# First norm of a macaron block: sums of squares by ScalarE over turned tokens, root on four numbers per token, spread by one product

## The chip, the core and the metric

One core of a Trainium2 chip runs the whole program; the other seven are idle. The metric is the device time of one execution in microseconds (us). The core's engines work through their own lists of instructions in order and meet at semaphores: PE (TensorE) multiplies matrices into PSUM, DVE (VectorE) and ACT (ScalarE) do the elementwise work, POOL (GpSimd) a little of it, and SP (SyncE) issues the DMA transfers.

## What is computed

One layer on 1,024 tokens of width 1,024, in float32: a half-step feed-forward block, a mixing part (short convolution and differential attention), a second half-step feed-forward block, and a last norm. The change touches the first lines only:

```python
def rms_norm(x, g):
    xf = x.astype(jnp.float32)
    y = xf * lax.rsqrt(jnp.mean(xf * xf, axis=-1, keepdims=True) + NORM_EPS)
    return (y * g.astype(jnp.float32)).astype(x.dtype)

def swiglu(x, w_gate, w_up, w_down):
    return (jax.nn.silu(x @ w_gate) * (x @ w_up)) @ w_down

h = h + 0.5 * swiglu(rms_norm(h, norm_ffn1[l]), ffn1_gate[l], ffn1_up[l], ffn1_down[l])
```

x is (1, 1024, 1024), the gate and up weights are (1024, 2816), the down weight (2816, 1024).

## The kernel before

The features lie on the partitions and the tokens along the free axis. The 1,024 tokens are two halves `t` of 512 and the 1,024 features two halves `o` of four blocks of 128, so the input is four tiles `h[o][t]` of 128 x 4 x 512. A product in float32 is made of three quick ones: each operand is split into a rounded part `hi` (an ACT copy) and the rest `lo` (a DVE subtraction), and hi x hi, hi x lo and lo x hi are summed in PSUM. A group is twelve such products of 128 x 128 by 128 x 512 (four blocks of features, three products each).

The width 2,816 of the feed-forward is worked in eleven steps `j` of 256 columns, gate and up together. Step 0 is written out by hand in `Start`, and its order on PE, DVE, ACT and POOL is the order of the code. It starts before the norm is known: `operand` multiplies x by the gain alone (ACT gives `hi`, DVE `lo`), `weights` splits a block of weights, `mm` adds one group of products, and only `ev` multiplies a finished sum in PSUM by the norm's factor `r[t]` of each token. There are sixteen groups, for gate and up (`x`), two column halves (`o`), two token halves (`t`) and two feature halves (`kk`). `squares` and `norm` make `r[t]`: ACT squares the eight 128 x 512 pieces of a token half, DVE adds them up (`add_square`), PE multiplies the sum with a matrix of ones, which adds over the partitions and gives every partition the result, and `rstd` takes the reciprocal root (one ACT operation, then three DVE operations of 128 x 512). `apply` (line 651) multiplies x by gain and `r[t]`: four DVE operations for each of the four tiles. These normed tiles are what all later steps multiply.

From step 1 on `pair_jobs` makes seven products in place of eight out of sums of quarters (a Strassen-like scheme): for each of gate and up the products come in the order `ORDER = (2, 1, 7, 6, 4, 5, 3)`, and each of them needs a block `B(i)`, a sum of normed tiles split into `hi` and `lo`. Products 1, 6, 5 and 3 are added one after the other onto one PSUM bank, 7 onto a second and 2 and 4 onto a third and back; after each of them the bank's value is taken out before the next product is added onto it:

```python
if (o, t) not in C:
    C[o, t] = self.C()
    nc.scalar.copy(C[o, t], ps)
else:
    nc.vector.tensor_tensor(C[o, t], C[o, t], ps, ALU.add)
```

The copy is line 308 (ACT), the addition line 310 (DVE). So product 6 can't begin until the addition of product 1 has read the bank, and that addition adds onto what the copy of product 2 took out. Outside the hand-written stretch the scheduler of the compiler sets the order of each engine's list. PSUM tiles are named `sc` (two tiles of two banks), `at` (two of one bank), `ps` and `ot` (one each); in SBUF, `Q` are the large tiles, `A` and `F` split weights, and `C` pieces of 128 x 512.

Of the kernel before, what the change touches and what calls it, by code (L numbers as in the profile page):

```python
# [25 lines left out]
EPS = 1e-6  # L26
# [34 lines left out]
class Operands:  # L61


    def __init__(self, k):
        self.k = k
        self.made = {}
        self.left = {}
# [62 lines left out]
class Stream(Operands):  # L130
# [29 lines left out]
class K:  # L160
# [293 lines left out]
    def setup(self):  # L454
        nc = self.nc
        self.cst = self.t("cst", [P, C_N])
        nc.sync.dma_start(self.cst, self.io["consts"])
        self.ones = self.t("ones", [P, P])
        nc.vector.memset(self.ones, 1.0)
        self.eps = self.t("eps", [P, 1])  # L460
        nc.vector.memset(self.eps, EPS)
        self.ng = self.t("ng", [P, 32])
        nc.vector.tensor_scalar(self.ng, self.cst[:, 0:32], -1.0, None, ALU.mult)

    def ffn_loads(self, wg, wu):
        return [self.load_raw(wg[0]), self.load_raw(wu[0])]
# [126 lines left out]
class Start:  # L593


    def __init__(self, k, x, wg, wu, gd):
        nc = k.nc
        self.k, self.gd = k, gd
        self.h = [[None, None], [None, None]]
        raws = [k.t("Q", [P, 2, 8, P]) for _ in range(2)]  # L600
        self.st, self.r, self.s, self.A, self.acc, self.G = {}, {}, {}, {}, {}, {}
        self.B = Blocks(k, 4)
        self.B.q = self.h
        dma = nc.sync.dma_start
        for kk in range(2):
            q = slice(4 * kk, 4 * kk + 4)
            h = self.h[kk][0] = k.t("Q", [P, 4, TH])
            dma(h[:, 0:2], x[kk][0][:, 0:2])
            dma(raws[0][:, 0, q], wg[:, 0, q])
            dma(h[:, 2:4], x[kk][0][:, 2:4])  # L610
            dma(raws[0][:, 1, q], wg[:, 1, q])
            for o in range(2):
                dma(raws[1][:, o, q], wu[:, o, q])
            self.s[kk, 0] = k.t("Q", [P, 4, TH], F32R), k.t("Q", [P, 4, TH], F32R)
        for kk in range(2):
            self.h[kk][1] = k.t("Q", [P, 4, TH])
            dma(self.h[kk][1], x[kk][1])
            self.s[kk, 1] = k.t("Q", [P, 4, TH], F32R), k.t("Q", [P, 4, TH], F32R)
        self.raws = raws
# [12 lines left out]
            nc.scalar.activation(hi[:, j], src, AF.Copy, scale=self.gain(o, j))  # L632
            nc.vector.scalar_tensor_tensor(lo[:, j], src, self.gain(o, j), hi[:, j].bitcast(F32), ALU.mult, ALU.subtract)

    def squares(self, o, t):
        k, nc = self.k, self.k.nc
        for j in range(4):
            sq = k.C()
            nc.scalar.activation(sq, self.h[o][t][:, j], AF.Square)
            k.add_square(self.st, t, sq)  # L640

    def norm(self, t):
        k, nc = self.k, self.k.nc
        ps = self.sc[1][:, :TH] if t == 0 else k.ps("at")
        nc.tensor.matmul(ps, k.ones, self.st[t][0], start=True, stop=True)
        self.r[t] = k.rstd(ps, D, TH)

    def apply(self, t, o):
        for j in range(4):
# [9 lines left out]
    def mm(self, x, o, t, kk):  # L659
        k = self.k  # L660
        if kk == 0:
            if t == 1 and x == 0:
                self.acc[x, o] = self.sc[1 - o][:, TH:]
            else:
                self.acc[x, o] = k.ps({(0, 1, 0): "ps", (0, 1, 1): "ot", (1, 1, 1): "ps"}.get((t, x, o), "at"))
        ps, a, (hi, lo) = self.acc[x, o], self.A[x, o, kk], self.s[kk, t]
        for q in range(4):
            for n, (y, z) in enumerate(((0, hi), (0, lo), (1, hi))):
                k.nc.tensor.matmul(ps, a[:, y, q], z[:, q], start=kk == q == n == 0, stop=kk == 1 and q == 3 and n == 2)

    def ev(self, x, o, t):
        k, nc = self.k, self.k.nc
        c = k.C()
        nc.vector.scalar_tensor_tensor(c, self.acc.pop((x, o)), -1.0, self.r[t], ALU.mult, ALU.mult)
        if x == 0:
            nc.scalar.activation(c, c, AF.Silu)
            self.G[o, t] = c
        else:
            g = self.G[o, t]
            k.tt(g, g, c, ALU.mult)  # L680
            k.finished(self.G, o, t, self.gd, 0)

    def run(self, load):
        k = self.k
        XO = [(0, 0), (0, 1), (1, 0), (1, 1)]
        B = self.B.get

        self.sc = [k.ps("sc"), k.ps("sc")]
        for _ in range(self.WARM):
            k.nc.tensor.matmul(self.sc[0][:, :P], k.ones, k.ones, start=True, stop=True)  # L690
        self.operand(0, 0, (0, 1))
        self.weights(0, 0, 0)
        self.operand(0, 0, (2, 3))
        self.mm(0, 0, 0, 0)
        for x, o in XO[1:]:
            self.weights(x, o, 0)
            self.mm(x, o, 0, 0)
        self.squares(0, 0)
        self.operand(1, 0, range(4))
        for o in range(2):  # L700
            self.weights(0, o, 1)
        self.mm(0, 0, 0, 1)
        self.squares(1, 0)
        for o in range(2):
            self.weights(1, o, 1)
        self.operand(0, 1, range(4))
        self.squares(0, 1)
        self.norm(0)
        self.mm(0, 1, 0, 1)
        self.operand(1, 1, range(4))  # L710
        self.squares(1, 1)
        raws = load()
        self.mm(1, 0, 0, 1)
        self.ev(0, 0, 0)
        self.ev(0, 1, 0)
        self.mm(1, 1, 0, 1)
        self.ev(1, 0, 0)
        self.ev(1, 1, 0)
        for x, o in XO[:2]:
            self.mm(x, o, 1, 0)  # L720
        self.apply(0, 0)
        self.norm(1)
        for x, o in XO[2:]:
            self.mm(x, o, 1, 0)
        B(1)
        self.apply(0, 1)
        self.mm(*XO[0], 1, 1)
        B(2)
        for x, o in XO[1:]:
            self.mm(x, o, 1, 1)  # L730
        self.apply(1, 1)
        for x, o in XO:
            self.ev(x, o, 1)
        self.apply(1, 0)
        self.B.plan(7)
        return raws

# [23 lines left out]
class Mixer:  # L761
# [10 lines left out]

    def constants(self):
        k, nc = self.k, self.k.nc
        self.ident = k.t("ident", [P, P])
        make_identity(nc, self.ident)

        mm = k.C()
        nc.gpsimd.memset(mm[:, 0:192], 0.0)
        nc.gpsimd.memset(mm[0:1, 0:64], 1.0)  # L780
        nc.gpsimd.memset(mm[0:1, 128:192], NEG_BIG)
        self.mask = k.t("msk", [P, 192], F32R)
        nc.vector.tensor_copy(self.mask, mm[:, 0:192])

        lam = k.C()
        lv = k.C()[:, 0:256]
        nc.sync.dma_start(lv, k.io["lambdas"])
        nc.vector.tensor_tensor(lam[:, 0:64], lv[:, 0:64], lv[:, 64:128], ALU.mult)
# [667 lines left out]
```

## Time and profile before

| | us |
|---|---|
| median of 3 runs (lowest, highest) | 2081.24 (2080.03, 2082.38) |
| the profiled execution, its own time | 2082.11 |
| its span from first to last instruction | 2080.3 |
| PE busy (share of the span) | 1981.0 (95%) |
| DVE busy | 1402.0 (67%) |
| ACT busy | 935.1 (45%) |

The times are of unprofiled executions, the rest is from one profiled execution; its own time is 1.8 us longer than its span. A busy share is a mean over the whole span and doesn't say what happens in the first 110 us, where the change lies. The granted clock of PE was 0.978 of 2.4 GHz on average.

### The profile page before, as it was taken

Reading aid. Unit: us, or ns where it says so; the run is one execution under the profiler, and the core shown is the slowest. Engines: PE = TensorE matmul, PEld = TensorE weight load, DVE = VectorE, ACT = ScalarE, POOL = GpSimd, SP = SyncE. Lnnn points to the kernel's source line nnn. Section 1 sums busy time; section 2 is a strip of 40 time slices with the busy share of each in tenths; the row PEclk is TensorE's granted clock in tenths of the full one; section 3 lists DMA queues with packets and bytes.
Section 4 is the critical chain, followed back from the end, with each engine's and each line's share of the span. In section 5 each row is a group of like instructions: output and inputs, shape, how many; then the busy total and the mean of one; then the engine's idle time right before and its main releaser. Section 6 shows DMA issues by size and latency. Waiting matters only on the chain.

```text
span 2080.3 us, 24145 instructions
## 1 busy us (share of the span) xinstructions
PE 1981.0 (95%) x8808; PEld 1624.7 (78%) x8808; DVE 1402.0 (67%) x2166; ACT 935.1 (45%) x1684; POOL 136.8 (7%) x123
## 2 busy tenths in 40 slices
PE   9799999999999999999799997999999999999997
PEld 8588888888877877777578775877788888888885
DVE  8965665676866856656376737798865665666874
ACT  7433333353464633233366656456433333353362
POOL 0000000000000000000244445000000000000000
PEclk9899999999999999999899998999999999999998
DMA  5223223264543423312333344423223223274441
GB/s 213 84 109 113 95 102 117 81 236 159 194 157 111 152 98 100 126 57 71 119 105 122 97 148 144 190 81 132 97 102 121 86 101 112 82 264 152 150 154 59
DMA packets 81208, 259.70 MB, mean 125 GB/s; under 512 B 10048, under 2 KB 16320, under 8 KB 63936
## 3 DMA queue, kind: packets, MB, share of 16 engines
q1 hardware_dynamic: 81088, 258.15, 34.8%
q8 instruction: 69, 1.13, 0.2%
q14 instruction: 51, 0.42, 0.1%
HBM read 183.14 MB, written 74.97 MB: 124 GB/s over the span
## 4 chain that ended last, share of the span: by engine, by line
PE 81%; DVE 10%; ACT 3%; issue 2%; POOL 1%; DMA 1%; SPq 0%; DVEq 0%; ACTq 0%; POOLq 0%
PE sc L267 37%; PE at L267 16%; PE ps L267 9%; PE ot L267 8%; DVE Q L243 3%; PE ps L1159 2%; DVE A L243 1%; DVE C L243 1%; DVE F L243 1%; PE ps L1221 1%; PE sc L955 1%; PE sc L339 1%; PE sc L338 1%; PE sc L337 1%; PE sc L1221 1%
## 5 line engine op out<-in xcount | busy, mean ns | idle before, releaser
L267 PE MATMUL sc<-Q,A 128*128 128x512 f32 x1968 | 473.5, 390 | 2.4 <-ACT C L308 2.4
L267 PEld LDWEIGHTS sc<-Q,A 128*128 128x128 f32 x1968 | 369.7, 188 | 81.3 <-ACT C L308 3.2
L267 PE MATMUL sc<-Q,F 128*128 128x512 f32 x1548 | 382.1, 396 | 29.5 <-ACT Q L248 11.4
L267 PEld LDWEIGHTS sc<-Q,F 128*128 128x128 f32 x1548 | 294.6, 191 | 96.9 <-ACT Q L248 12.9
L243 DVE TENSOR_TENSOR F<-Q,F 128x512 fp32r<-128x512 f32 (+1 forms) x307 | 211.8, 696 | 170.1 <-ACT F L248 169.7
L248 ACT CAST F<-Q 128x512 fp32r<-128x512 f32 (+1 forms) x315 | 190.0, 612 | 256.5 <-PE sc L267 88.1
L243 DVE TENSOR_TENSOR Q<-Q,Q 128x512 fp32r<-128x512 f32 (+4 forms) x334 | 278.7, 887 | 33.6 <-ACT Q L248 26.8
L248 ACT CAST A<-Q 128x512 fp32r<-128x512 f32 (+1 forms) x299 | 180.3, 611 | 268.0 <-PE sc L267 159.1
L243 DVE TENSOR_TENSOR A<-Q,A 128x512 fp32r<-128x512 f32 (+1 forms) x299 | 202.0, 678 | 130.2 <-ACT A L248 129.3
L267 PE MATMUL at<-Q,F 128*128 128x512 f32 x1128 | 279.4, 393 | 10.1 <-ACT C L308 9.2
L267 PEld LDWEIGHTS at<-Q,F 128*128 128x128 f32 x1128 | 213.0, 189 | 57.3 <-ACT C L308 10.9
L248 ACT CAST Q<-Q 128x512 fp32r<-128x512 f32 (+1 forms) x214 | 153.1, 759 | 87.0 <-DVE Q L243 31.1
L243 DVE TENSOR_TENSOR C<-C,C 128x512 f32<-128x512 f32 x236 | 161.5, 688 | 16.6 <-DMA C<-zd 5.0
L243 DVE TENSOR_TENSOR Q<-Q 128x512 f32<-128x512 f32 x216 | 148.3, 690 | 3.7
L267 PE MATMUL ps<-Q,A 128*128 128x512 f32 x498 | 124.2, 390 | 0.0
L308 ACT COPY C<-sc 128x512 f32<-128x512 f32 x88 | 51.4, 588 | 156.5 <-PE sc L267 155.4
L267 PE MATMUL ot<-Q,A 128*128 128x512 f32 x450 | 112.8, 392 | 0.9 <-DVE Q L398 0.9
L267 PEld LDWEIGHTS ps<-Q,A 128*128 128x128 f32 x498 | 93.6, 188 | 19.6 <-issue 0.3
L1159 PE MATMUL ps<-Q,F 128*128 128x512 f32 x384 | 105.9, 412 | 3.1 <-ACT C L1165 3.1
L267 PE MATMUL at<-Q,A 128*128 128x512 f32 x444 | 107.6, 389 | 0.8 <-DVE C L310 0.8
L310 DVE TENSOR_TENSOR C<-C,sc 128x512 f32<-128x512 f32 x81 | 55.6, 687 | 75.3 <-ACT C L308 35.1
L267 PEld LDWEIGHTS ot<-Q,A 128*128 128x128 f32 x450 | 85.3, 190 | 19.0 <-issue 1.3
(218 smaller groups left out, 2190.6 us busy)
## 6 DMA issues: line engine op xcount, KB each, us to landing
Q<-in_ffn_gate SPq DMA_DIRECT2D x21, 1024.0 KB, 5.8
Q<-in_ffn_up SPq DMA_DIRECT2D x21, 1024.0 KB, 4.8
Q<-in_w_in SPq DMA_DIRECT2D x20, 1024.0 KB, 5.4
g1d<-C SPq DMA_DIRECT2D x77, 256.0 KB, 2.0
g2d<-C SPq DMA_DIRECT2D x77, 256.0 KB, 2.0
Q<-in_ffn_down SPq DMA_DIRECT2D x16, 1024.0 KB, 6.5
Q<-g1d SPq DMA_DIRECT2D x14, 1024.0 KB, 6.3
Q<-g2d SPq DMA_DIRECT2D x14, 1024.0 KB, 5.8
```

The source lines that it names most:

```text
L243: e.tensor_tensor(out, a, b, op)
L248: self.nc.scalar.copy(hi, src)
L267: mm = lambda *x, **kw: self.nc.tensor.matmul(*x, skip_group_check=True, **kw)
L308: nc.scalar.copy(C[o, t], ps)
L310: nc.vector.tensor_tensor(C[o, t], C[o, t], ps, ALU.add)
L337: mm(ps, a[:, 0, q], hi[:, q], start=n == q == 0, stop=False)
L338: mm(ps, a[:, 0, q], lo[:, q], start=False, stop=False)
L339: mm(ps, a[:, 1, q], hi[:, q], start=False, stop=n == 1 and q == 3)
L955: nc.tensor.matmul(sc[:, a : a + w], qs[:, hl, s, qb * P : (qb + 1) * P], kst[:, s, a : a + w], start=hl == 0, stop=hl == 1 and a + w < n)
L1159: nc.tensor.matmul(ps, a[kk][:, x, q], y[:, q], start=c == 0, stop=c == 23)
L1221: nc.tensor.matmul(ps, a[:, x, kk], b[:, y, kk % 2], start=c == 0, stop=c == 11)
```

## The change

`squares` no longer squares the pieces as they lie. PE turns them first (a transpose of 128 x 128 by the unit matrix `ident`, which is now made at the start), so that 128 tokens lie on the partitions and their 1,024 features along the free axis of one `sc` tile; one ACT operation squares the 1,024 values of each token and sums them into one number. There are eight such steps, four blocks `b` of 128 tokens for each half `t`, with eight turns each. `root` takes the reciprocal root on 128 x 4 numbers (one ACT and four small DVE operations) and then ACT multiplies `ident` by the four columns (four operations of 128 x 128) into a tile `diag`. `norm` multiplies this tile with the matrix of ones, which gives all partitions the factor of each token, and ACT copies it out of PSUM. The order of `run` is another one: all eight groups of the first token half and all turns come before the first `ev`.

```diff
-    def squares(self, o, t):
-        for j in range(4):
-            sq = k.C()
-            nc.scalar.activation(sq, self.h[o][t][:, j], AF.Square)
-            k.add_square(self.st, t, sq)
+    def squares(self, t, b):
...
+        tp = k.ps("sc")
+        for o in range(2):
+            for j in range(4):
+                c = (4 * o + j) * P
+                nc.tensor.transpose(tp[:, c : c + P], self.h[o][t][:, j, b * P : (b + 1) * P], k.ident)
+        nc.scalar.activation(self.junk, tp, AF.Square, accum_out=self.w[t][:, 0, b : b + 1])
+
+    def root(self, t):
+        ss, y, v, a, r = (self.w[t][:, i] for i in range(5))
+        nc.scalar.activation(y, ss, AF.Abs_reciprocal_sqrt, bias=k.eps, scale=1.0 / D)
+        nc.vector.tensor_scalar(v, ss, 0.5 / D, 0.5 * EPS, ALU.mult, ALU.add)
+        nc.vector.tensor_tensor(a, y, y, ALU.mult)
+        nc.vector.tensor_tensor(v, a, v, ALU.mult)
+        nc.vector.scalar_tensor_tensor(r, v, -1.5, y, ALU.add, ALU.mult)
+        d = self.diag[t] = k.C()
+        for b in range(4):
+            nc.scalar.activation(d[:, b * P : (b + 1) * P], k.ident, AF.Copy, scale=r[:, b : b + 1])
 
     def norm(self, t):
         ps = self.sc[1][:, :TH] if t == 0 else k.ps("at")
-        nc.tensor.matmul(ps, k.ones, self.st[t][0], start=True, stop=True)
-        self.r[t] = k.rstd(ps, D, TH)
+        nc.tensor.matmul(ps, k.ones, self.diag[t], start=True, stop=True)
+        self.r[t] = k.C()
+        nc.scalar.copy(self.r[t], ps)
...
         self.mm(0, 0, 0, 1)
-        self.squares(1, 0)
+        self.squares(0, 0)
+        self.squares(0, 1)
         for o in range(2):
             self.weights(1, o, 1)
+        self.mm(0, 1, 0, 1)
+        self.squares(0, 2)
+        self.squares(0, 3)
         self.operand(0, 1, range(4))
-        self.squares(0, 1)
+        self.root(0)
+        self.mm(1, 0, 0, 1)
+        self.squares(1, 0)
+        self.squares(1, 1)
+        self.operand(1, 1, range(4))
+        self.mm(1, 1, 0, 1)
+        self.squares(1, 2)
+        self.squares(1, 3)
+        raws = load()
+        self.sc = [k.ps("sc"), k.ps("sc")]
         self.norm(0)
-        self.mm(0, 1, 0, 1)
-        self.operand(1, 1, range(4))
-        self.squares(1, 1)
-        raws = load()
-        self.mm(1, 0, 0, 1)
-        self.ev(0, 0, 0)
-        self.ev(0, 1, 0)
-        self.mm(1, 1, 0, 1)
-        self.ev(1, 0, 0)
-        self.ev(1, 1, 0)
+        self.root(1)
         for x, o in XO[:2]:
             self.mm(x, o, 1, 0)
+        for x, o in XO:
+            self.ev(x, o, 0)
+        for x, o in XO[:2]:
+            self.mm(x, o, 1, 1)
+        self.apply(0, 1)
+        B(2)
+        self.mm(*XO[2], 1, 0)
+        self.norm(1)
...
```

What this does to the lists of the engines is seen at three places. Names are tile kinds with running numbers, and the numbers differ between the two programs.

On PE before, the product with ones for the first token half (line 645) stands between the fifth and the sixth group of `Start`:

```order
L669 MATMUL at_22_156<-Q_12_114,F_33_236 128x512
L669 MATMUL at_22_156<-Q_11_113,F_33_236 128x512
L645 MATMUL sc_20_124<-C_29_217,ones_2_87 128x512
L669 MATMUL at_24_172<-Q_11_113,A_34_239 128x512
L669 MATMUL at_24_172<-Q_12_114,A_34_239 128x512
```

On PE now, the same product (line 668, on the tile `diag`) stands behind the eighth group (`ot`, line 693) and the last sixteen of the 64 turns (line 648):

```order
L693 MATMUL ot_28_208<-Q_13_119,A_36_272 128x512
L693 MATMUL ot_28_208<-Q_12_118,A_36_272 128x512
L648 MATMUL sc_43_378<-ident_5_93,Q_14_120 128x128 x4
L648 MATMUL sc_43_378<-ident_5_93,Q_17_124 128x128 x4
L648 MATMUL sc_44_388<-ident_5_93,Q_14_120 128x128 x4
L648 MATMUL sc_44_388<-ident_5_93,Q_17_124 128x128 x4
L668 MATMUL sc_48_403<-C_39_320,ones_2_87 128x512
L693 MATMUL sc_48_403<-Q_15_122,F_21_153 128x512
```

The product moved behind three more groups and all turns, and its PSUM tile `sc_48` lies where `sc_43` lay, so it waits for the square of that tile.

On DVE before, the end of the first half's norm (lines 437 to 439), the operand of the last tile (633), the last additions of squares (243 on `C`) and the first `ev` (674):

```order
L437 SCALAR_TENSOR_TENSOR C_46_293<-sc_20_124,C_45_292 128x512
L438 TENSOR_TENSOR C_46_293<-C_46_293,C_45_292 128x512
L439 SCALAR_TENSOR_TENSOR C_46_293<-C_46_293,C_45_292 128x512
L633 SCALAR_TENSOR_TENSOR Q_18_122<-Q_16_119,cst_1_85,Q_17_121 128x512 x4
L243 TENSOR_TENSOR C_41_280<-C_41_280,C_47_318 128x512
L243 TENSOR_TENSOR C_41_280<-C_41_280,C_48_321 128x512
L243 TENSOR_TENSOR C_41_280<-C_41_280,C_49_324 128x512
L243 TENSOR_TENSOR C_41_280<-C_41_280,C_50_327 128x512
L674 SCALAR_TENSOR_TENSOR C_53_346<-at_22_156,C_46_293 128x512
```

On DVE now, the same place, with the first `ev` in line 698:

```order
L635 SCALAR_TENSOR_TENSOR Q_19_127<-Q_17_124,cst_1_85,Q_18_126 128x512 x4
L656 TENSOR_SCALAR tn_40_337<-tn_40_337 128x4
L657 TENSOR_TENSOR tn_40_337<-tn_40_337 128x4
L658 TENSOR_TENSOR tn_40_337<-tn_40_337 128x4
L659 SCALAR_TENSOR_TENSOR tn_40_337<-tn_40_337 128x4
L698 SCALAR_TENSOR_TENSOR C_51_441<-at_22_160,C_49_405 128x512
```

The additions and the wide root are gone; the small root of the second token half (its inputs are the last squares) now stands ahead of the first `ev`.

On DVE before, the first two additions of line 310, those of product 1 in step 1, with `apply` of the last tile (line 651) ahead of them and the making of `B(7)` (243 on `Q`) behind:

```order
L243 TENSOR_TENSOR C_72_525<-C_54_349,C_71_524 128x512
L651 SCALAR_TENSOR_TENSOR Q_13_115<-Q_13_115,ng_4_91,C_59_403 128x512 x4
L310 TENSOR_TENSOR C_81_572<-C_81_572,sc_86_598 128x512
L310 TENSOR_TENSOR C_84_591<-C_84_591,ps_90_632 128x512
L243 TENSOR_TENSOR Q_13_115<-Q_16_119,Q_13_115 128x512 x4
```

On DVE now, the same two additions:

```order
L243 TENSOR_TENSOR C_68_583<-C_63_553,C_51_441 128x512
L243 TENSOR_TENSOR Q_103_818<-Q_8_102,Q_102_817 128x512 x3
L243 TENSOR_TENSOR Q_107_867<-Q_17_124,Q_106_866 128x512 x4
L243 TENSOR_TENSOR Q_103_818<-Q_8_102,Q_102_817 128x512
L243 TENSOR_TENSOR C_69_584<-C_52_444,C_68_583 128x512
L310 TENSOR_TENSOR C_78_627<-C_78_627,sc_83_653 128x512
```

They stand behind the making of all the blocks (`Q_103` and `Q_107` are the `lo` parts of `B(5)` and `B(3)`, the last two). Between the first `ev` and the first of these additions there were 62 DVE instructions, and now there are 96.

## Rows read from the trace of the kernel before

**Rows 1.** The page: the chain that ended last, shares of the span by engine.

```profile
PE 81%; DVE 10%; ACT 3%; issue 2%; POOL 1%; DMA 1%; SPq 0%; DVEq 0%; ACTq 0%; POOLq 0%
```

**Rows 2.** Busy us by engine (xinstructions) in stretches; PE's granted clock, DMA share, GB/s.

```profile
70.00:80.00 10.00, 1.22 (x2) 0.50 (x2) 9.97 (x17) 3.26 (x6) 0.00 (x0) 0.60 0.21 79
80.00:90.00 10.00, 9.53 (x31) 7.69 (x32) 10.00 (x18) 5.87 (x11) 0.00 (x0) 0.72 0.07 26
100.00:400.00 300.00, 300.00 (x1325) 248.51 (x1324) 188.02 (x290) 108.81 (x190) 0.00 (x0) 1.00 0.29 109
```

**Rows 3.** The chain that ended last, in order of time: start us, us, what.

```profile
7.71 0.65 DVE Q L633
...
79.80 0.63 ACT Q L248
```

**Rows 4.** Timeline of PE: start us, us, instruction, [idle before <- releaser].

```profile
20.33 2.88 PE L669 MATMUL at<-Q,F 128*128 128x512 f32 x12
...
26.64 2.88 PE L669 MATMUL ps<-Q,F 128*128 128x512 f32 x12
29.36 2.88 PE L669 MATMUL ot<-Q,A 128*128 128x512 f32 x12
...
77.45 0.79 PE L267 MATMUL sc<-Q,F 128*128 128x512 f32 x1 [9.39 <-ACT Q L248]
```

**Rows 5.** Timeline of DVE.

```profile
18.82 3.08 DVE L243 TENSOR_TENSOR C<-C,C 128x512 f32<-128x512 f32 x4
...
35.56 1.28 DVE L674 SCALAR_TENSOR_TENSOR C<-at,C 128x512 f32<-128x512 f32 x2
...
40.69 2.73 DVE L651 SCALAR_TENSOR_TENSOR Q<-Q,ng,C 128x512 f32<-128x512 f32 x4
...
43.34 0.69 DVE L437 SCALAR_TENSOR_TENSOR C<-at,C 128x512 f32<-128x512 f32 x1
...
74.87 0.68 DVE L310 TENSOR_TENSOR C<-C,sc 128x512 f32<-128x512 f32 x1
...
79.08 14.53 DVE L243 TENSOR_TENSOR Q<-Q,Q 128x512 f32<-128x512 f32 x24
```

**Rows 6.** Products of line 267, the first 180 of them: PE, PEld, clock, DMA.

```profile
54.70:112.30 57.60, 44.39 (x180) 35.41 (x180) 0.88 0.25 91
```

**Rows 7.** Timeline of PE in the attention: four turns, and what follows them.

```profile
1077.83 0.63 PE L1001 MATMUL at<-ident,Q 128*128 128x128 f32 x4
1078.21 1.63 PE L1159 MATMUL ps<-Q,F 128*128 128x512 f32 x6
```

**Rows 8.** Timeline of ACT in `Start`.

```profile
20.20 2.57 ACT L632 ACTIVATE Q<-Q,cst 128x512 fp32r<-128x512 f32 x4
...
22.66 2.19 ACT L639 ACTIVATE C<-Q 128x512 f32<-128x512 f32 x4
...
24.87 1.28 ACT L436 ACT_TABLE_LOAD   x1
...
37.61 1.15 ACT L676 ACTIVATE C<-C 128x512 f32<-128x512 f32 x2
```

**Rows 9.** Timeline of ACT in the attention: an activation with a sum, and what follows.

```profile
1167.17 1.11 ACT L973 ACTIVATE Q<-sc,sm 128x1024 f32<-128x1024 f32 x1
...
1168.28 0.61 ACT L943 CAST A<-C 128x512 fp32r<-128x512 f32 x1
```

**Rows 10.** Small tiles by line: ns min/median/max, first and last start us.

```profile
L972 ACT ACTIVATE sm<-sm x64: 197/203/225, 1030.2 to 1226.5; 128x1 f32<-128x1 f32 x64
L988 DVE TENSOR_TENSOR sm<-sm,nlam x32: 158/160/1033, 1037.8 to 1227.5; 128x1 f32<-128x1 f32 x32
```

**Rows 11.** Groups by line: busy us, mean ns of one | idle before.

```profile
L248 ACT CAST A<-at 128x128 fp32r<-128x128 f32 x16 | 4.3, 266 | 8.4 <-DVE A L243 8.4
L308 ACT COPY C<-sc 128x512 f32<-128x512 f32 x88 | 51.4, 588 | 156.5 <-PE sc L267 155.4
```

**Rows 12.** Busy us by engine in a stretch around the second feed-forward's start.

```profile
1340.00:1500.00 160.00, 149.43 (x633) 120.46 (x633) 140.84 (x224) 87.18 (x152) 0.00 (x0) 0.98 0.27 99
```

More of the change, by code (lines that the diff above doesn't have):

```diff
@@ L463, in setup @@
         nc.vector.tensor_scalar(self.ng, self.cst[:, 0:32], -1.0, None, ALU.mult)
+        self.ident = self.t("ident", [P, P])
+        make_identity(nc, self.ident)
     def ffn_loads(self, wg, wu):
@@ L600, in __init__ @@
         raws = [k.t("Q", [P, 2, 8, P]) for _ in range(2)]
-        self.st, self.r, self.s, self.A, self.acc, self.G = {}, {}, {}, {}, {}, {}
+        self.w, self.diag, self.r, self.s, self.A, self.acc, self.G = {}, {}, {}, {}, {}, {}, {}
         self.B = Blocks(k, 4)
@@ L633, in operand @@
             nc.vector.scalar_tensor_tensor(lo[:, j], src, self.gain(o, j), hi[:, j].bitcast(F32), ALU.mult, ALU.subtract)
-    def squares(self, o, t):
+    def squares(self, t, b):
         k, nc = self.k, self.k.nc
-        for j in range(4):
-            sq = k.C()
-            nc.scalar.activation(sq, self.h[o][t][:, j], AF.Square)
-            k.add_square(self.st, t, sq)
+        if (t, b) == (0, 0):
+            self.junk = k.t("Q", [P, D])
+        if b == 0:
+            self.w[t] = k.t("tn", [P, 5, 4], bufs=2)
+        tp = k.ps("sc")
[5 more added lines that the diff above has]
+    def root(self, t):
+        k, nc = self.k, self.k.nc
+        ss, y, v, a, r = (self.w[t][:, i] for i in range(5))
[7 more added lines that the diff above has]
+            nc.scalar.activation(d[:, b * P : (b + 1) * P], k.ident, AF.Copy, scale=r[:, b : b + 1])
     def norm(self, t):
@@ L662, in mm @@
             if t == 1 and x == 0:
-                self.acc[x, o] = self.sc[1 - o][:, TH:]
+                self.acc[x, o, t] = self.sc[1 - o][:, TH:]
             else:
-                self.acc[x, o] = k.ps({(0, 1, 0): "ps", (0, 1, 1): "ot", (1, 1, 1): "ps"}.get((t, x, o), "at"))
-        ps, a, (hi, lo) = self.acc[x, o], self.A[x, o, kk], self.s[kk, t]
+                self.acc[x, o, t] = k.ps({(0, 1, 0): "ps", (0, 1, 1): "ot", (1, 1, 1): "ps"}.get((t, x, o), "at"))
+        ps, a, (hi, lo) = self.acc[x, o, t], self.A[x, o, kk], self.s[kk, t]
         for q in range(4):
@@ L673, in ev @@
         c = k.C()
-        nc.vector.scalar_tensor_tensor(c, self.acc.pop((x, o)), -1.0, self.r[t], ALU.mult, ALU.mult)
+        nc.vector.scalar_tensor_tensor(c, self.acc.pop((x, o, t)), -1.0, self.r[t], ALU.mult, ALU.mult)
         if x == 0:
@@ L686, in run @@
         B = self.B.get
-        self.sc = [k.ps("sc"), k.ps("sc")]
+        warm = k.ps("sc")
         for _ in range(self.WARM):
-            k.nc.tensor.matmul(self.sc[0][:, :P], k.ones, k.ones, start=True, stop=True)
+            k.nc.tensor.matmul(warm[:, :P], k.ones, k.ones, start=True, stop=True)
         self.operand(0, 0, (0, 1))
@@ L697, in run @@
             self.mm(x, o, 0, 0)
-        self.squares(0, 0)
         self.operand(1, 0, range(4))
@@ L702, in run @@
         self.mm(0, 0, 0, 1)
-        self.squares(1, 0)
+        self.squares(0, 0)
+        self.squares(0, 1)
         for o in range(2):
             self.weights(1, o, 1)
+        self.mm(0, 1, 0, 1)
+        self.squares(0, 2)
+        self.squares(0, 3)
         self.operand(0, 1, range(4))
-        self.squares(0, 1)
-        self.norm(0)
-        self.mm(0, 1, 0, 1)
-        self.operand(1, 1, range(4))
-        self.squares(1, 1)
-        raws = load()
-        self.mm(1, 0, 0, 1)
-        self.ev(0, 0, 0)
-        self.ev(0, 1, 0)
-        self.mm(1, 1, 0, 1)
-        self.ev(1, 0, 0)
-        self.ev(1, 1, 0)
+        self.root(0)
[8 more added lines that the diff above has]
+        self.sc = [k.ps("sc"), k.ps("sc")]
+        self.norm(0)
+        self.root(1)
         for x, o in XO[:2]:
             self.mm(x, o, 1, 0)
-        self.apply(0, 0)
-        self.norm(1)
-        for x, o in XO[2:]:
[L724 to L732, printed above, removed]
+        for x, o in XO:
[6 more added lines that the diff above has]
+        self.norm(1)
+        self.mm(*XO[3], 1, 0)
+        self.apply(0, 0)
+        B(1)
+        self.mm(*XO[2], 1, 1)
+        self.apply(1, 1)
+        for x, o in XO[:2]:
+            self.ev(x, o, 1)
+        self.mm(*XO[3], 1, 1)
+        self.apply(1, 0)
+        for x, o in XO[2:]:
             self.ev(x, o, 1)
-        self.apply(1, 0)
         self.B.plan(7)
@@ L774, in constants @@
         k, nc = self.k, self.k.nc
-        self.ident = k.t("ident", [P, P])
-        make_identity(nc, self.ident)
+        self.ident = k.ident
         mm = k.C()
```

## The prediction

> **What bounds the kernel now.** I read the page's chain first: PE carries 81% of it and DVE 10% [rows 1]. The chain in time says where DVE's part lies: it runs over DVE from 7.7 us without a break of note until it passes to an ACT cast at 79.80, and PE's product comes from that cast [rows 3]. The stretches say the same from PE's side. From 70 to 80 PE works 1.2 of 10 us at a granted clock of 0.60, while DVE is full; from 80 to 90 the clock is still 0.72; from 100 to 400 PE has no gap at all [rows 2]. PE's longest wait there, 9.39 us, ends at 77.45 with the first product that needs the block B(7) [rows 4]. So a gain or loss of the first 110 us goes whole into the total, as later there is no slack on PE that could take it up. As a mark I use the first 180 products of line 267: before, they are through at 112.3 us [rows 6]. The prediction is the time at which the same 180 are through in the changed program.
>
> **What is removed and added.** DVE loses 14 additions of squares and six wide root operations; four additions that depend on one another last 3.08 us with 0.69 for the last, so one step is (3.08 - 0.69) / 3 = 0.80; in the run of 24 independent operations a step is (14.53 - 0.69) / 23 = 0.602 [rows 5]. So 20 operations are worth 12.0 to 16.0 us, by the dependence nearer to 16. DVE gets eight operations on 128 x 4 numbers at 0.16 each by the nearest row [rows 10], 1.3 us, and is relieved of 10.7 to 14.7. PE gets 64 turns. Four of them of the same form take 0.38 us until the next product starts [rows 7], 0.095 each, 6.1 us in all; were a turn as slow as 128 columns of the two-pass product with ones (that product adds 26.64 - 20.33 - 2 x 2.72 = 0.87 us for 512 columns [rows 4]), it would be 0.22. ACT loses 16 squares at (2.19 - 0.6) / 3 = 0.53 and two wide roots, and gets eight squares of 128 x 1024 with a sum. The nearest row, an exponential of that size with a sum, takes 1.11 us from its start to the next operation's [rows 9]; bounds are 2 x 0.53 = 1.06 and, without any overlap, 1.30. I take 1.11, since that row has the same size, source and sum. ACT also gets two roots on four columns (0.20 [rows 10]), eight products of `ident` (0.27 each from the nearest 128 x 128 row [rows 11], some 0.2 when they overlap, as larger ones do) and two copies of 0.59 [rows 11].
>
> **When the first `ev` can start.** Before, it starts at 35.56 [rows 5]. Now the factor comes by a longer way, which I follow through the lists.
> - The fifth group still ends at 23.05 (20.33 and one group, 29.36 - 26.64 = 2.72 [rows 4]), as its operands only come sooner. Then sixteen turns, 1.52, to 24.57; the sixth group to 27.29; eight turns, the last of which ends 0.9 later: 28.2. PE works on, and ACT can square the third block.
> - From here ACT works alone and PE waits for it, since the two `sc` tiles are both full until ACT has squared them. Its list: six squares, 6 x 1.11 = 6.7; the operands of the two tiles of the second token half, 8 x 0.615 = 4.9 ((22.66 - 20.20) / 4 [rows 8]); one table load, 1.28 [rows 8]; two roots, 0.4; twice a wait for the three dependent small DVE operations of `root`, 2 x 0.6; the four products for the first half, 0.8; the copy of the factor, 0.6. Sum 15.9, so 28.2 + 15.9 = 44.1.
> - The small root of the second half stands ahead of the first `ev` on DVE, and it is in this sum. The first `ev` starts at 44.1, 8.5 us later than before.
>
> Bounds: squares at 1.06, 43.8; at 1.30, 45.2; turns at 0.22 (24 of them lie between 23.05 and 28.2), 3.0 more. So 43.8 to 48.2. PE's 6.1 us of turns cost nothing else: behind its eighth group PE waits for ACT from 35.8 to 43 with pauses only for turns. DVE's relief falls mostly ahead of 44, where DVE now waits for ACT; behind the first `ev` only the second wide root is gone (three operations, 1.8 us).
>
> **From the first `ev` to PE's release.** Product 6 of step 1 adds onto the bank of product 1 and has to wait until the DVE addition of line 310 has read it. Between the first `ev` and that addition there were 62 DVE instructions, and now there are 96, because the blocks B(7), B(6), B(4), B(5) and B(3) are now all made ahead of it. Check of the method on before: with the first `ev` 63 instructions, 16 of them `apply` at 0.6625 ((43.34 - 40.69) / 4 [rows 5]) and 47 at 0.602, are 38.9 us, and 35.56 + 38.9 = 74.5; the trace has the addition at 74.87 [rows 5]. Now 97 instructions, 81 x 0.602 + 16 x 0.6625 = 59.4, and about 0.9 us for a wait: the first product of gate and up needs the Silu, and ACT makes it 0.8 (the second half's products of `ident`) + 1.28 (table) + 0.63 after the first `ev`, while DVE has three `ev`s of 0.62 to do. So the addition starts at 44.1 + 59.4 + 0.9 = 104.4 and PE may go on at 105.1.
>
> ACT gives the same picture. The copy of product 2 (line 308), which the addition adds onto, and which also releases the tile for product 7 of the gate, stands on ACT behind the casts of B(6), B(4), B(5) and B(3). The last of these needs a DVE result that comes eleven instructions ahead of the addition, so the copy runs at about 98 to 99. PE, which is through with products 2, 1 and 7 of `up` at about 85.5, waits until then, does product 7 of the gate (12 products, at half speed 5 us) and waits again until 105.1.
>
> **The sum.** Behind 105.1 lie 108 of the 180 products (72 are those of blocks 2, 1 and 7). At 2.72 / 12 = 0.227 us [rows 4] they take 24.5: 129.6. I find no wait in between that lasts longer than PE has work: the next copies and additions come at 106 and later, one per group of 2.72. 129.6 - 112.3 = 17.3 us. The profiled execution has 2082.1 (span 2080.3 and 1.8 around it), with 17.3 it is 2099.4; the median of the runs is 0.9 below that execution, so I predict 2098.5, in round figures 2099 us.
>
> Two costs I put at nothing. The transfers for step 2 are now queued on SP behind the first two writes of step 0, at some 49 us in place of 41; they are wanted after 110 us, and without that cover a transfer of 1 MB would be late by that 8 us. And the scheduler's order also changes a little between 1340 and 1500 us, where PE lost 160 - 149.4 = 10.6 us before [rows 12]. I can't price it; by this row it can give back at most 10.6, and I allow 5 either way.
>
> **The rivals.**
> - *DVE is relieved and the kernel gets faster.* The chain runs over DVE for 72 us, and up to 14.7 us of it are removed. PE can get back no more than it lost there, the wait of 9.4 us [rows 4] and about 10 x (1 - 0.72) = 2.8 us of low clock [rows 2]: 2081.2 - 12.2 = 2069, or 2075 where the turns' 6.1 us find no cover. For this the first `ev` must start by about 25 us, with 62 instructions up to the addition. It decides from where the addition starts before 104.4 - 17.3 = 87.1. Against it: `ev` stands behind all squares in the lists. The Trainium skill, "Perfetto Trace Analysis", section "Identifying the Most-Contended Engine", speaks for this rival: find the engine with the highest occupancy in the regime and optimize it first. In that sense the engine of this stretch is DVE (9.97 of 10 us [rows 2]), and taking work off it should pay; the trace agrees on the engine, and no row of before can show whether the lighter DVE is let start.
> - *No change.* The late start would have to be made good, for instance by a delay that PE's waits of before (9.4 us at 77) cover. PE's list has those waits still, only later. It would need the addition at 87.
> - *Slower, but by the late start alone*, if the 34 instructions moved ahead of the addition held nobody up: 8.5 - 1.8 = 6.7 us, 2088. Against it: product 6 can't begin without the addition.
> - *Heavier.* Turns at 0.22 and squares at 1.30 (4.1 us), and PE at half speed for a while behind each of its longer waits, as at 77 (1 to 2 us): 2104; with 5 more from the second place 2109.
>
> **Chances and range.** The forecast as it stands, 2093 to 2104 (2099 with the unknown place and the lower bounds either way): 0.74. Heavier, above 2104: 0.10. The late start alone, 2085 to 2093: 0.07. No change, within 0.2% (4.2 us, about what a measurement of this kernel can tell from none): 0.05. Faster: 0.04. So slower 0.91. The range from 2091 to 2107 leaves out about 2 in 10.
>
> **What would show it.** Right: the first `ev` at 43 to 46 us; PE nearly idle from 36 to 43 and from 86 to 99, with a granted clock near 0.5 behind the second gap; the first addition of line 310 at 103 to 107; 180 products of line 267 through at 128 to 132; no gap on PE from there to 400. Each turn near 0.1 us and each square near 1.1 us on ACT. Wrong: if ACT squares much faster, or finds work that I put behind it, the first `ev` comes sooner; if the addition comes before 87, the sign is wrong; if the 180 products are through at 130 and the time is still not near 2099, the stretch from 1340 to 1500 has moved.

## The result, and the profile after

The changed kernel takes 2102.03 us (median of 4 runs, 2097.73 to 2104.02), the kernel before 2080.95 beside it: a ratio of 1.0098 (95% interval 1.0080 to 1.0115). The profiled execution took 2104.02 us with a span of 2102.2, 21.9 more than before. One execution of the later kernel e6, of 2510.68 us at a granted clock of 0.747, is left out of its median and ratio below.

The first `ev` starts later and the first addition of line 310 much later. DVE's timeline (start, length, instruction, in brackets the idle time before and who ended it) answers to [rows 5]:

```profile
39.67 2.74 DVE L635 SCALAR_TENSOR_TENSOR Q<-Q,cst,Q 128x512 fp32r<-128x512 f32 x4 [4.17 <-ACT Q L634]
...
45.92 1.28 DVE L698 SCALAR_TENSOR_TENSOR C<-at,C 128x512 f32<-128x512 f32 x2
...
89.56 4.92 DVE L243 TENSOR_TENSOR Q<-Q,Q 128x512 f32<-128x512 f32 x8
...
107.01 0.72 DVE L310 TENSOR_TENSOR C<-C,sc 128x512 f32<-128x512 f32 x1
```

The first `ev` moved from 35.56 to 45.92, the addition from 74.87 to 107.01. DVE, which shows no pause from 9 us to the first `ev` before, now waits for ACT. Its waits from 9 to 46 us by who ended them (us in all, times, longest):

```profile
DVE F L243 <- ACT F L248: 9.6, 1, 9.6
DVE Q L635 <- ACT Q L634: 8.1, 3, 4.2
DVE tn L657 <- ACT tn L655: 2.3, 2, 1.6
DVE tn L656 <- ACT Q L649: 1.2, 1, 1.2
```

That is 21.2 us. The stretches of ten us show where it lies (busy us of PE, PEld, DVE, ACT, POOL, then PE's granted clock, the DMA engines' busy share and GB/s; PEld is PE's loading of weights):

```profile
30.00:40.00 10.00, 8.63 (x54) 7.07 (x52) 3.64 (x9) 9.26 (x18) 0.00 (x0) 1.00 0.00 0
40.00:50.00 10.00, 6.97 (x17) 4.23 (x16) 5.57 (x13) 8.08 (x16) 0.00 (x0) 0.66 0.01 2
...
80.00:90.00 10.00, 6.09 (x23) 4.08 (x23) 10.00 (x18) 4.60 (x8) 0.00 (x0) 1.00 0.01 4
90.00:100.00 10.00, 0.00 (x0) 0.00 (x0) 10.00 (x18) 5.53 (x10) 0.00 (x0) 0.51 0.20 77
100.00:110.00 10.00, 7.70 (x22) 5.64 (x23) 9.11 (x16) 4.26 (x9) 0.00 (x0) 0.64 0.35 125
```

From 30 to 50 ACT is nearly full (17.3 of 20 us) while DVE has less than half to do; from 80 to 107 it is the other way round, and PE stands still from 90 to 100. PE's timeline names the two gates, and the slow product ahead of the factor, answering to [rows 4]:

```profile
42.52 2.07 PE L668 MATMUL sc<-C,ones 128*128 128x512 f32 x2 [2.35 <-ACT Q L649]
...
101.72 5.49 PE L267 MATMUL sc<-Q,F 128*128 128x512 f32 x12 [13.67 <-ACT C L308]
107.78 3.00 PE L267 MATMUL sc<-Q,F 128*128 128x512 f32 x12 [0.58 <-DVE C L310]
```

The last of the first 180 products of line 267 starts at 132.2 us, where it started at 112.2, at the end of the stretch of [rows 6]; from 140 to 400 PE has no gap:

```profile
69.80:132.20 62.40, 44.54 (x180) 34.91 (x181) 0.86 0.23 85
...
140.00:400.00 260.00, 260.00 (x1149) 215.29 (x1148) 159.74 (x245) 93.34 (x163) 0.00 (x0) 1.00 0.27 102
```

So 20.0 of the 21.9 us are lost by then.

### The profile page after: what moved, and what is told of

Same layout as the page of the kernel before. It is cut to its first block, busy times and chain, and to the rows that moved or that the text cites. A ratio compares the mean times of both kernels' runs of the same rounds, so it can differ in the third digit from the quotient of the medians.

```text
span 2102.2 us, 24269 instructions
## 1 busy us (share of the span) xinstructions
PE 1992.3 (95%) x8872; PEld 1632.2 (78%) x8872; DVE 1392.8 (66%) x2154; ACT 936.3 (45%) x1692; POOL 136.8 (7%) x123
## 4 chain that ended last, share of the span: by engine, by line
PE 81%; DVE 10%; ACT 4%; issue 2%; POOL 1%; DMA 1%; SPq 0%; DVEq 0%; ACTq 0%; POOLq 0%
PE sc L267 36%; PE at L267 16%; PE ps L267 9%; PE ot L267 8%; DVE Q L243 4%; PE ps L1190 3%; DVE F L243 1%; PE ps L1252 1%; PE sc L986 1%; DVE A L243 1%; PE sc L337 1%; PE sc L339 1%; PE sc L338 1%; PE ot L1062 1%; DVE C L243 1%
## 5 line engine op out<-in xcount | busy, mean ns | idle before, releaser
L267 PE MATMUL sc<-Q,F 128*128 128x512 f32 x1548 | 377.5, 394 | 27.5 <-ACT C L308 13.7
L243 DVE TENSOR_TENSOR C<-C,C 128x512 f32<-128x512 f32 x224 | 153.3, 688 | 16.5 <-DMA C<-zd 4.9
L1190 PE MATMUL ps<-Q,F 128*128 128x512 f32 x384 | 107.7, 417 | 3.0 <-ACT C L1196 3.0
```

The source lines that it names most:

```text
L243: e.tensor_tensor(out, a, b, op)
L1190: nc.tensor.matmul(ps, a[kk][:, x, q], y[:, q], start=c == 0, stop=c == 23)
```

## The experiments

For each kernel three marks are read from its profile as above: the start of the first `ev`, the start of the first addition of line 310, and the start of the 180th product of step 1 and after. DVE's waits are counted from 9 us to the first `ev` and from there to the addition. Times are medians. Ratios are against the kernel before in the same runs, where its medians were 2080.95 (beside the changed kernel), 2082.85 (e1 to e4), 2080.94 (e5 to e8) and 2081.22 (e9, e10); they can differ from the quotient of two medians by up to 0.0004.

| kernel | time us | ratio (95% interval) | first `ev` | addition | DVE waits, us | 180th product |
|---|---|---|---|---|---|---|
| before | 2080.95 | 1 | 35.56 | 74.87 | 0 + 0.2 | 112.2 |
| changed | 2102.03 | 1.0098 (1.0080 to 1.0115) | 45.92 | 107.01 | 21.2 + 1.5 | 132.2 |
| e1 | 2108.17 | 1.0121 (1.0106 to 1.0137) | 45.21 | 88.92 | 20.2 + 5.7 | 136.6 |
| e2 | 2094.11 | 1.0051 (1.0034 to 1.0067) | 36.96 | 101.51 | 0.8 + 3.1 | 126.4 |
| e3 | 2109.38 | 1.0126 (1.0110 to 1.0143) | 52.72 | 113.84 | 27.9 + 1.5 | 139.0 |
| e4 | 2086.68 | 1.0020 (1.0010 to 1.0031) | 31.46 | 77.86 | 9.9 + 5.7 | 115.1 |
| e5 | 2094.57 | 1.0065 (1.0050 to 1.0080) | 45.45 | 86.08 | 20.2 + 2.9 | 125.3 |
| e6 | 2079.39 | 0.9995 (0.9983 to 1.0007) | 29.66 | 74.21 | 7.8 + 3.9 | 110.3 |
| e7 | 2086.99 | 1.0035 (1.0022 to 1.0049) | 29.45 | 78.08 | 7.7 + 7.6 | 117.6 |
| e8 | 2102.27 | 1.0105 (1.0087 to 1.0123) | 48.29 | 109.22 | 23.5 + 1.5 | 134.4 |
| e9 | 2078.14 | 0.9987 (0.9978 to 0.9997) | 29.34 | 73.56 | 7.7 + 2.6 | 107.7 |
| e10 | 2081.89 | 1.0002 (0.9993 to 1.0010) | 29.55 | 74.06 | 7.4 + 5.3 | 112.4 |

The last column less 112.2 is each kernel's loss in time (ratio less 1, times 2081) within 2 us, but for e2, where it is 14.2 against 10.6; e2's profiled execution was the slowest of its four, with a span 14.7 above that of before. So most of the matter is decided in the first 140 us. A mark is read from one execution, though, and behind it single executions still differ: the one of e3 is 26.8 us behind at the mark and 22.0 at the end of its span.

**e1: step 1 in the order of the code.** A region written out by hand is laid around the jobs of step 1.

```diff
+            hand = ExitStack()
             for n, (p, r) in enumerate(jobs):
+                if j == j0 == 1 and n == 0:
+                    hand.enter_context(self.tc.manual_schedule(engines=BYHAND))
...
                 self.submit(p, r)
+            hand.close()
```

> The changed kernel, but the jobs of step 1 are kept in the order of the code on PE, DVE, ACT and POOL (the region written out by hand reaches to the last job of step 1). The first addition of line 310 then stands 58 DVE instructions behind the first `ev` in place of 96, and the copies of line 308 stand ahead of the casts of B(6), B(4), B(5) and B(3). Nothing else of the change is touched. Theory (late start and the place of the addition): the first `ev` stays near 45.9 us, the first addition comes at 45.9 + 59 x 0.612 + 0.9 = 83 in place of 107. If PE then never waits again, its 120 products behind that point are through at about 112 and the time is 2082. If DVE can't make the later blocks faster than PE eats them (they are needed soon anyhow: B(7), B(6), B(4), B(5) and B(3) are 97 instructions in any order, through at 105 to 110), the 180 products are through at 122 to 124 and the time is 2092 to 2094. Rival (only the late start counts, the order of the blocks holds nobody up): no change, 2102.

Both theories missed. The addition came 18 us sooner and the kernel is slower still. The order of the code makes a block piece by piece, sum, cast, `lo`, so that DVE waits for ACT and ACT for DVE at each piece, 1.98 us for what took 1.2; PE gets its products in ones and twos, and its clock from 100 to 110 is 0.66. DVE's timeline, and a stretch of all engines:

```profile
82.37 1.29 DVE L247 TENSOR_TENSOR Q<-Q,Q 128x512 fp32r<-128x512 f32 x2 [0.68 <-ACT Q L252]
84.35 1.29 DVE L247 TENSOR_TENSOR Q<-Q,Q 128x512 fp32r<-128x512 f32 x2 [0.69 <-ACT Q L252]
```
```profile
100.00:110.00 10.00, 9.38 (x23) 6.06 (x23) 6.50 (x11) 4.38 (x8) 0.00 (x0) 0.66 0.00 0
```

**e5: the same, blocks in fours.** All four sums of a block stand ahead of its four casts and four `lo` parts:

```diff
-            for dst, a, b, sign in B_STEPS.get(i, ()):
-                d, a, b = (self.q[x][t][:, c, :] for x, t in (dst, a, b))
-                k.tt(d, a, b, ALU.add if sign > 0 else ALU.subtract)
+            for e in range(self.nk) if self.whole and c == 0 else () if self.whole else (c,):
+                for dst, a, b, sign in B_STEPS.get(i, ()):
+                    d, a, b = (self.q[x][t][:, e, :] for x, t in (dst, a, b))
+                    k.tt(d, a, b, ALU.add if sign > 0 else ALU.subtract)
```

> The kernel of e1_step1_by_hand, but the sums of a block's four pieces stand together and then the four casts and the four `lo` parts (in e1 each piece waited 0.69 us for its own cast, and ACT each time for DVE). Theory of the prediction (34 instructions ahead of the first addition of line 310 are a loss of their own): the addition comes at about 84 to 86 in place of 107 and the time falls to 2084 to 2088. Second theory (DVE's whole list is the bound, so that what is not made ahead of the addition is missing behind it): the blocks B(6), B(4), B(5) and B(3) come at 95, 103 and up to 118, PE waits for each of them, and the time is 2094 to 2101, little better than the changed kernel.

2094.57: the second theory. With the start of `ev` left as it is, bringing the addition forward by 21 us gives back 6.9 of the 20.0 us at the last mark. The other 13.1 stay, now as waits for the blocks themselves: the products with B(5) start at 107.77 and stop for DVE. PE's timeline:

```profile
107.77 0.50 PE L273 MATMUL sc<-Q,F 128*128 128x512 f32 x1 [0.53 <-ACT Q L254]
...
110.73 0.96 PE L273 MATMUL sc<-Q,F 128*128 128x512 f32 x3 [2.23 <-DVE Q L249]
```

**e2: the order without the method.** The changed order of `run`, with the sums of squares of before:

```diff
+    def squares(self, t, b):
+        o = b // 2
+        for j in (2 * (b % 2), 2 * (b % 2) + 1):
+            sq = k.C()
+            nc.scalar.activation(sq, self.h[o][t][:, j], AF.Square)
+            k.add_square(self.st, t, sq)
+    def root(self, t):
+        pass
```

`norm` and its wide root are those of before too.

> The order of `run` of the changed kernel, but the sums of squares of before (pieces squared by ACT as they lie, added by DVE, one product with ones, wide root); no turns, no `ident` products. The first addition of line 310 stands 99 DVE instructions behind the first `ev`. Theory (the order, not the method, puts the blocks ahead of the addition): first `ev` at 36 to 38, the first addition at 37 + 100 x 0.607 + 0.9 = 98.5, 180 products through at 123 to 124, time 2092 to 2094: slower than before although the method of the norm is the old one. Rival (the new method of the norm is the whole loss): 2081, as before.

As the theory said, but for an addition 3.0 us later than worked out, of which 2.2 are waits of DVE behind the first `ev` (3.1 where I had 0.9). With the old method, a first `ev` only 1.4 us late and 99 instructions ahead of the addition the kernel loses 14.2 us at the last mark. The order alone is a loss, and the copy of line 308 stands late in it as in the changed kernel. PE's timeline:

```profile
96.18 5.10 PE L267 MATMUL sc<-Q,F 128*128 128x512 f32 x12 [12.97 <-ACT C L308]
```

**e3: each square twice.** The cleanest test of the late start: nothing but ACT's chain is longer.

```diff
-        nc.scalar.activation(self.junk, tp, AF.Square, accum_out=self.w[t][:, 0, b : b + 1])
+        for _ in range(2):
+            nc.scalar.activation(self.junk, tp, AF.Square, accum_out=self.w[t][:, 0, b : b + 1])
```

> The changed kernel with each of the eight ACT squares of 128 x 1024 done twice (same result), all else as it is; 96 instructions between the first `ev` and the first addition as before this edit. Theory (ACT's chain sets the first `ev`, and all behind it is one DVE list without slack): six of the eight squares lie behind 28.2 us, so the first `ev` comes 6 x 1.11 = 6.7 later, at 52.6, the first addition at 113.7, and the time is 2108 to 2109. Rival (the first `ev` is late but DVE or PE takes it up, the loss comes from the place of the addition alone): within 2 us of the changed kernel, 2102 to 2104.

The three marks move by 6.80, 6.83 and 6.8 us, the ratio by 0.0028 (5.8 us). Nothing takes a delay of the factor up. DVE's timeline:

```profile
52.72 1.28 DVE L699 SCALAR_TENSOR_TENSOR C<-at,C 128x512 f32<-128x512 f32 x2
...
113.84 0.67 DVE L310 TENSOR_TENSOR C<-C,sc 128x512 f32<-128x512 f32 x1
```

**e8: each turn twice.** `for o in range(2)` around the turns becomes `for o in (0, 1, 0, 1)`.

> The changed kernel with all 64 turns done twice (same result). Theory (turns are hidden behind ACT's chain, but for those between the fifth group and the third square): 24 more turns at 0.095 to 0.104 ahead of the third square, first `ev` 2.3 to 2.5 later, time 2104 to 2105. Rival (turns cost PE their full time): 6.1 to 6.7 us more, 2108 to 2109. Turns cost nothing at all: 2102.

The marks move by 2.37, 2.21 and 2.2 us, as expected of the turns between the fifth group and the third square; the other forty cost nothing. The median (2102.27) doesn't show it: the changed kernel's four runs lie 6.3 us apart, so that only the marks, each from one execution, speak for it.

**e4, e6, e9: the method in another order.** e4 puts the turns of the first half between the second and fourth group and the first `ev` ahead of the squares of the second half. The product with `diag` gets an `sc` tile of its own, and the two Silu of the first half come behind the third `ev`. The core of `run` in e4:

```python
self.squares(0, 0)
self.squares(0, 1)
self.mm(*XO[2], 0, 0)
...
self.squares(0, 2)
self.squares(0, 3)
self.mm(*XO[3], 0, 0)
self.root(0)
self.mm(0, 0, 0, 1)
...
self.norm(0)
self.mm(0, 1, 0, 1)
self.operand(0, 1, range(4))
self.ev(0, 0, 0)
self.squares(1, 0)
self.squares(1, 1)
self.apply(0, 0)
```

> The new method (turns, ACT squares with a sum, root on 128 x 4, product with `diag`), but in an order close to that of before: the turns of the first token half lie between the second and the fourth group, where ACT was idle, the product with `diag` behind the fifth group, and the first `ev` ahead of the squares of the second half. The second half's turns follow groups six and seven. 67 DVE instructions stand between the first `ev` and the first addition, eight of them work that stood ahead of the first `ev`. Theory (the loss is one of place, not of the method): first `ev` at 27 to 30, first addition at 70 to 74, PE bound by its own work of 68 + 6 us or B(7) at 75 to 77, so the time is 2072 to 2080. Rival (64 turns on PE and the longer way to the factor cost their time wherever they stand): 2085 or more.

A miss: 2086.68, slower than before. DVE is relieved, but waits 9.9 us up to the first `ev` (the longest, 2.53, for a square of the first half) and 5.7 behind it; the four `lo` parts of the second half's first tile, 2.74 us, also stood ahead of the first `ev`, and PE's next product comes at 80.44. Therefore e6:

```diff
+        self.operand(0, 1, range(4))
         self.squares(0, 2)
...
-        self.operand(0, 1, range(4))
         self.ev(0, 0, 0)
+        self.apply(0, 0)
         self.squares(1, 0)
         self.squares(1, 1)
-        self.apply(0, 0)
-        raws = load()
         self.ev(0, 1, 0)
+        self.apply(0, 1)
+        self.operand(1, 1, range(4))
+        raws = load()
         self.mm(1, 0, 0, 1)
         self.squares(1, 2)
         self.squares(1, 3)
-        self.operand(1, 1, range(4))
+        B(1)
+        B(2)
         self.root(1)
...
```

> As e4_new_sums_early, with DVE's and ACT's lists rearranged so that DVE finds work where it waited in e4 (16.5 us of waits from 7.6 to 79.8): the operand of the first tile of the second half ahead of the last two squares of the first half, `apply` of both tiles of the first half behind the first `ev`, B(1) and B(2) ahead of the second root, the product with `diag` of the second half behind group (1,0,1,0). Theory (the relief of DVE counts as far as DVE doesn't wait): first `ev` at 29 to 30, B(7) and with it PE's next product at 73 to 76 in place of 77.45 and 80.44, time 2072 to 2078. Rival (the turns' 6 us and the longer way are paid in any place): 2084 to 2088.

Also a miss: 2079.39, by the ratio as fast as before and not faster. DVE still waits 11.7 us in all. e9 takes out what is left behind the first `ev`:

```diff
         self.squares(1, 3)
-        B(1)
-        B(2)
         self.root(1)
...
         self.ev(1, 1, 0)
+        B(1)
+        B(2)
```

and each Silu stands right behind its `ev`.

> As e6_new_sums_early_2, but the Silu of the first piece stands in ACT's gap of 3.04 us at 30 us, the second root ahead of the casts of B(1) and B(2), and those blocks behind the `ev`s of the first token half. In e6 DVE waited 1.17, 0.30 and 2.43 us behind the first `ev`; here I expect 1 to 2.5 us in all. If DVE's waits are what kept e6 from being faster than before, PE's next product comes at 75.5 to 77 in place of 78 and the time falls by 1 to 3 us, to 2077 to 2080. If not, 2080 to 2082.

2078.14, as expected. The new method is here faster than before by 0.13%, with an interval that ends just below 1 (0.9997), and faster than the changed kernel by some 23 us. From the changed kernel it differs in the order and in the `sc` tile of its own only. It is the best of three orders, and so thin an edge is weak evidence of a gain. PE still pauses once for B(7):

```profile
74.05 0.39 PE L267 MATMUL ot<-Q,A 128*128 128x512 f32 x1
76.71 1.07 PE L267 MATMUL sc<-Q,F 128*128 128x512 f32 x3 [2.28 <-DVE Q L243]
```

**e7: e6 with step 1 by hand in fours.**

> The kernel of e6 with step 1 in the order of the code and blocks in fours as in e5. If the automatic order of e6 is good (blocks made without gaps), this adds waits between DVE and ACT and is 3 to 10 us slower than e6: 2078 to 2086. If the early addition of line 310 is worth something by itself, it is faster than e6: 2068 to 2072.

2086.99, 7.6 us slower than e6 and just above the range given. In e6 the automatic order has the addition early already (74.21); by hand it comes at 78.08, and DVE's waits behind the first `ev` grow from 3.9 to 7.6 us.

**e10: e9 with four `lo` parts on GpSimd.**

```diff
+            if (o, t) == (1, 1):
+                u = self.k.C()
+                nc.gpsimd.tensor_scalar(u, src, self.gain(o, j), None, ALU.mult)
+                nc.gpsimd.tensor_tensor(lo[:, j], u, hi[:, j].bitcast(F32), ALU.subtract)
+            else:
+                nc.vector.scalar_tensor_tensor(lo[:, j], src, self.gain(o, j), hi[:, j].bitcast(F32), ALU.mult, ALU.subtract)
```

> As e9, and the four `lo` parts of the last tile of the second token half (4 x 0.61 us of DVE) are made by GpSimd in two operations each (a product with the gain and a difference, by the trace 0.73 and 1.35 us); they are wanted by PE only at some 55 us. 61 DVE instructions in place of 68 stand between the first `ev` and the first addition of line 310. If DVE's list is the bound up to PE's next product, this comes 2.4 us sooner than in e9, and with PE's slow stretch behind its wait (about 3 us) gone the time is 2073 to 2077, below both kernels. If PE's own work is the bound (it has 74.1 us of products and turns up to there), no more than 1 us below e9.

A miss: 2081.89, slower than e9. The 2.4 us were taken from DVE at a place where the next thing in its list is the second root, which waits for ACT's last square in any case: the wait there is 3.83 us in place of 1.18. DVE also stands still beside GpSimd (last section), and the addition comes at 74.06 in place of 73.56. The lost time is made larger on PE. After two waits for B(7) its products go on at 80.21, where in e9 they went on at 76.71, and its clock from 80 to 90 is 0.69 in place of 0.96:

```profile
76.05 0.50 PE L267 MATMUL sc<-Q,F 128*128 128x512 f32 x1 [1.89 <-ACT Q L248]
...
80.21 1.65 PE L267 MATMUL sc<-Q,F 128*128 128x512 f32 x3 [3.43 <-DVE Q L243]
```

## Why the prediction held, and what in it did not

**The first `ev`.** Forecast 44.1, measured 45.92. The parts held: a square with its sum takes 1.02 and 0.19 us, 1.14 from one to the next (forecast 1.11), a turn (24.63 - 22.97) / 16 = 0.104 (0.095). One was missing: the sum has no term for the product with `diag`. At the 0.87 us of the product with ones it would have ended within ACT's last square. It came behind a wait of PE, and in a stretch of low clock (0.66 from 40 to 50) took 2.07 us, so ACT's copy waited 1.01 us. PE's timeline with sixteen turns, then ACT's:

```profile
22.97 1.91 PE L648 MATMUL sc<-ident,Q 128*128 128x128 f32 x16
24.63 2.99 PE L693 MATMUL at<-Q,A 128*128 128x512 f32 x12
```

```profile
24.04 1.02 ACT L649 ACTIVATE Q<-sc 128x1024 f32<-128x1024 f32 x1 [7.79 <-PE sc L648]
24.96 0.19 ACT L649 ACTIVATION_READ_ACCUMULATOR Q<-sc 128x1 f32 x1
25.18 1.03 ACT L649 ACTIVATE Q<-sc 128x1024 f32<-128x1024 f32 x1
...
44.63 0.59 ACT L670 COPY C<-sc 128x512 f32<-128x512 f32 x1 [1.01 <-PE sc L668]
```

e8 shows the other side: with more turns PE had no long wait there, its clock from 40 to 50 stayed at 1.00 and the product took 1.12:

```profile
45.84 1.12 PE L668 MATMUL sc<-C,ones 128*128 128x512 f32 x2 [0.38 <-ACT Q L649]
```

**From the `ev` to the addition.** Forecast 60.3 us for 97 instructions and a wait, measured 61.1; the wait was 1.5 and not 0.9. The copy of line 308 released PE at 101.72 (98 to 99), the addition at 107.78 (105.1). The 2.6 us by which the sum was short (132.2 against 129.6) are the 1.8 of the first `ev` and the 0.8 of this stretch, and they are nearly all by which 2099 fell short of 2102.

**The rivals.** "Late start alone" (2088) fell: the time is 2102, and e2, with hardly a late start, loses 14 us at the last mark. "Heavier" was right in its second half, a slow clock behind PE's waits. "DVE is relieved and the kernel gets faster" was rejected for this order, rightly. e9 shows that with the new method the kernel can be 0.13% faster than before; no run has e9's order with the old sums, so how much of that comes from DVE's relief isn't shown. The Trainium skill, "Perfetto Trace Analysis", section "Optimization Strategy", says how to go on once the engine is known: find its gaps, see which semaphore each waits on, and let that dependency start sooner or end faster. The trace agrees: from e4 over e6 to e9, where gaps of DVE were closed in this way, DVE's waits fall from 15.7 over 11.7 to 10.3 us and the last mark from 115.1 over 110.3 to 107.7. By the section of the Trainium skill that the prediction cites for this rival, work taken off DVE should pay; in the changed order it didn't (2102.03 against 2080.95), and the measurement decides.

**How the loss divides** is what the prediction had too simple. It priced the late start alone at 6.7 us (2088), which leaves 10.6 of its 17.3 us to the place of the addition, one behind the other. The runs show two causes that overlap. The place without the late start (e2) loses 14.2 us at the last mark, the late start without the place (e5, with the waits of the hand order in it) 13.1, both together 20.0. I read this as PE waiting for whichever comes last; no run shows it apart from the hand order's own waits. The blocks are needed soon in any order, so that moving the addition ahead of them gives back less than the 21 us by which it moves.

Most of the loss is the order's, but not all of it. From e2 to the changed kernel only the method differs, and it costs 5.8 us more at the last mark (9.8 by the two ratios), since in this order the new method makes the first `ev` 9.0 us later. In e9's order the same turns, squares and small roots are 4.5 us ahead of before at the last mark.

**The rest of the program.** I allowed 5 us either way for 1340 to 1500. The same work now lies some 20 us later, from 1360 to 1520, and PE lost 160 - 148.4 = 11.6 us there, 1.1 more than the 10.6 of before [rows 12]. That is over half of the 1.9 us that are lost behind the last mark:

```profile
1360.00:1520.00 160.00, 148.36 (x628) 119.03 (x627) 142.01 (x227) 86.69 (x152) 0.00 (x0) 0.98 0.27 99
```

The transfers for step 2, issued at 51.84, kept nobody waiting; from there to 140 us the timelines of PE, DVE and ACT show no wait for a transfer.

## What to carry to other kernels

Taking work off the engine that sets the end is worth what that engine doesn't then wait for. Ask of each piece of work that is removed what stood behind it in the list, whether that can start sooner, and on which engine the replacement stands; here 10.7 to 14.7 us of work went from DVE by the prediction's count, and 21.2 us of waiting for ACT came in. When a mark early in the program (here the 180th product) tells the whole time, compare kernels by it as well: in e3 and e8 it moved by what was changed, where the total moves by several us from run to run.

## What the runs showed of the hardware

- The same wait can leave PE fast or slow. In both kernels a group behind a wait of 2.59 us for the same copy of line 308 took 4.50 us in one execution, at a granted clock of 0.63, and 3.04 in the other, at 1.00. PE ran the same groups without a gap ahead of the wait in both. Of the kernel before, then of the changed one:

```profile
809.46 4.50 PE L267 MATMUL at<-Q,F 128*128 128x512 f32 x12 [2.59 <-ACT C L308]
```
```profile
828.61 3.04 PE L267 MATMUL at<-Q,F 128*128 128x512 f32 x12 [2.59 <-ACT C L308]
```

- DVE operations were held up while GpSimd ran a difference of two tiles. In e10 DVE's last small root operation took 1.28 us in place of 0.16 and ended at 43.26, with GpSimd's difference of 41.95 to 43.25:

```profile
41.98 1.28 DVE L664 SCALAR_TENSOR_TENSOR tn<-tn 128x4 f32<-128x4 f32 x1
```
```profile
41.95 1.30 POOL L638 TENSOR_TENSOR Q<-C,Q 128x512 fp32r<-128x512 f32 x1
```

The Trainium skill, "GPSIMD Engine Reference", section "Specifications", lists the SBUF interfaces as shared with VectorE, with contention where a DVE instruction has two SBUF inputs, among other cases. The trace agrees for the difference, and for the operation of 0.16 us it is a price of 1.12. It doesn't agree for every operation of GpSimd: beside its product of one tile with a column (43.22 to 44.79) a DVE addition of two SBUF tiles took its usual 0.69:

```profile
43.90 0.69 DVE L243 TENSOR_TENSOR C<-C,C 128x512 f32<-128x512 f32 x1
```

- A product of GpSimd with a column of gains took 1.57 us here; the 0.73 that I used for it in e10's expectation is that of line 981 in the attention, which works in place and with a second factor of 1.0. Why it is shorter isn't shown.
